# A second group of seven in the last feed-forward's up product, with both groups' weight sums made in DRAM by accumulating transfers

## The chip, the cores and the metric

The kernel runs on one core of a Trainium2 chip. The metric is the device time of one launch in microseconds (us), lower is better. Each kernel is run several times, and the median is given with the lowest and the highest.

## The reference

A two-layer encoder trunk on 256 rows of 1024 numbers, in float32. Each layer adds half a gated feed-forward, a token mixer (a causal depthwise convolution in the first layer, latent attention in the second), and another half feed-forward; an RMSNorm stands before each and at the end. There are four feed-forwards in all, and the last one is where the change lies.

```python
D_MODEL, SEQ, DEPTH, D_FF, FFN_RES_WEIGHT = 1024, 256, 2, 2816, 0.5

def rmsnorm(x, g):
    return x * lax.rsqrt(jnp.mean(x * x, axis=-1, keepdims=True) + RMS_EPS) * g

def swiglu_ffn(h, w1, w3, w2):
    return (jax.nn.silu(h @ w1) * (h @ w3)) @ w2

def reference(x, ...):
    h = x
    for i in range(DEPTH):
        h = h + FFN_RES_WEIGHT * swiglu_ffn(rmsnorm(h, ffn_norm1[i]), ffn1_w1[i], ffn1_w3[i], ffn1_w2[i])
        m = rmsnorm(h, mix_norm[i])
        h = h + (conv_module(m, ...) if i == 0 else mla(m, positions, ...))
        h = h + FFN_RES_WEIGHT * swiglu_ffn(rmsnorm(h, ffn_norm2[i]), ffn2_w1[i], ffn2_w3[i], ffn2_w2[i])
    return rmsnorm(h, final_norm)
```

## The kernel before, in words

**Numbers in two parts.** TensorE multiplies with operands of type fp32r, which hold fewer bits than float32. The kernel writes each float32 operand as a high part, the value cast to fp32r, and a low part, the rest. A product is three matmuls: rows high by weight low, high by high, low by high (`mm3`, lines 330 to 336; the three matmul lines are L332, L335 and L336).

**Weight blocks.** Weights come from DRAM in blocks of 128 x 2048 float32 (1 MB). A list, `blocks`, holds the order of use; `load` (L218) fetches the next block with a transfer of SyncE's queue (SP) into one of four `raw` buffers, ScalarE casts it to `hi` in two halves (L246) and VectorE subtracts to `lo` in two halves (L247). There are five pairs of `hi` and `lo`. `weights` hands out the next block and calls `load_ahead`, which has already written out the loads of the next three (four within a group of seven). Which instruction stands where in an engine's queue is decided when the kernel is built, by a scheduler with priorities; at run time each engine takes its queue in that order.

**A feed-forward.** `ffn_in` (L834) goes over the 2816 columns in six chunks `c`: five of 512 and one of 256. An ordinary chunk has four blocks, two for the first matrix (m=0) and two for the second (m=1), and each block serves both halves of the rows (tb=0 and 1): 2 x 2 x 8 products of `mm3`, 96 matmuls. Then come for each tb the SiLU on ScalarE (L948), the gate's product on VectorE (L950), and `turn`: a 32x32 transpose on VectorE (L470), four stores to DRAM (L474) and one read back (L479) by SP, and the high and low parts `Gh` and `Gl` (L845).

**A group of seven.** Four blocks (two by two) times two by two of rows is eight products of 12 matmuls. With Strassen's scheme (Winograd's form) it is seven, of sums of rows by sums of blocks: 84 matmuls. `SEVEN_UP` says which chunks are done so: chunk 3 of feed-forwards 1, 2 and 3 (0 is the first, 3 the last). The down product has a group of seven too (`SEVEN_DOWN`). The parts of it:

- `load_seven` (L189) fetches the four blocks (`fetched`, L182), makes four sums of them on VectorE in the raw buffers (`sub` in L204 to L210, recorded at its inner line L200), and splits each of the seven operands by L214 (ScalarE) and L200 (VectorE).
- `whole_rows` (L349) adds the rows' high and low parts, `sums_of_rows` (L344) makes four sums of them, and `forms_of` splits those (L361, L362). This runs two chunks before the group.
- `seven_products` (L366) runs the products in order and adds them up in four accumulators, with copies by ScalarE and two additions by VectorE (both recorded at the helper's line L258).

Instructions called through `urgent` get a high priority, and `behind` (L158) places a group's casts, subtractions and sums after the last six urgent ones of their engine. The gate's products of a chunk in `seven_up`, and of the chunk before it, are urgent. `fetched` and `load` place a load behind the last store that was placed so (`turns`).

**The ends of the stage before.** The MLA mixer's norms leave their last GpSimd operation at L1454; the norm of the last feed-forward has its last one at L519, `rh`, half the factor by which the down product's result is added. The final norm's operations (L724) come behind the down product.

## Time and profile before

| | |
|---|---|
| median of 3 runs | 900.82 us (898.79, 901.63, 900.82) |
| the profiled execution's own time | 902.66 us |
| its span in the trace | 900.9 us, mean granted clock 0.998 |
| TensorE busy | 890.0 us, 99% |
| VectorE busy | 743.2 us, 83% |
| ScalarE busy | 571.8 us, 63% |
| GpSimd busy | 104.9 us, 12% |
| transfers | 198.94 MB, mean 221 GB/s; SP's queue takes 61.2% of the 16 engines' span |

The table is from one profiled execution. The span runs from the first to the last recorded instruction; the execution's own time has the start and end around it. Busy shares are means over the whole span, while the change touches one stretch of it: the last feed-forward begins at about 730 us and its down product ends shortly before the final norm's operation at 888.15. Times in quoted rows are microseconds from the start of the span. A row of a timeline gives the start, the length, the engine, the line, the operation, output and inputs, the count (a row with x2 joins two instructions that follow each other), and in brackets the idle time before it with what ended it.

### The profile page before, as it was taken

What the parts mean: (1) busy time and instruction counts of PE and PEld (TensorE: products, weight loads), DVE (VectorE), ACT (ScalarE), POOL (GpSimd) and SP (SyncE); (2) the same over time, 40 slices, a digit from 0 to 9 for tenths busy, and PEclk for the clock granted to TensorE, in tenths of its full rate; (3) what the DMA queues carried; (4) which work ended last, traced back from release to release, by engine and by line L of the source; (5) the groups of instructions that cost most, each with busy time, mean ns of one, the idle gap of its engine ahead of it and who ended that gap; (6) DMA issues with size and microseconds to landing.
All of it is one profiled execution on the core that took longest, in us unless ns stands there. A gap on an engine that the chain in (4) does not pass through costs nothing.

```text
span 900.9 us, 12238 instructions
## 1 busy us (share of the span) xinstructions
PE 890.0 (99%) x4221; PEld 745.7 (83%) x4221; DVE 743.2 (83%) x1083; ACT 571.8 (63%) x993; POOL 104.9 (12%) x227
## 2 busy tenths in 40 slices
PE   9999999999999999999999999999999999999997
PEld 7888887898988888878888888788899888888886
DVE  6787779579998998899588989994768579999963
ACT  7966468388877645666375566564767576374752
POOL 1000000069962000000010000000400010000000
PEclk9999999999999999999999999999999999999999
DMA  9987629734315864939759369396545449377451
GB/s 333 363 313 282 212 69 335 295 125 171 105 57 207 291 241 154 368 98 356 283 167 331 136 206 354 98 384 219 198 165 178 150 141 352 99 287 293 169 200 47
DMA packets 71054, 198.94 MB, mean 221 GB/s; under 512 B 12368, under 2 KB 41936, under 8 KB 51664
## 3 DMA queue, kind: packets, MB, share of 16 engines
q1 hardware_dynamic: 70560, 197.47, 61.2%
q8 instruction: 33, 0.54, 0.2%
q10 hardware_dynamic: 432, 0.69, 0.2%
q14 instruction: 29, 0.24, 0.1%
HBM read 181.87 MB, written 16.25 MB: 220 GB/s over the span
## 4 chain that ended last, share of the span: by engine, by line
PE 82%; DVE 7%; DMA 6%; ACT 2%; issue 2%; SPq 0%; POOL 0%; DVEq 0%; ACTq 0%
PE u L336 13%; PE u L332 13%; PE u L335 13%; PE o L332 8%; PE o L336 8%; PE o L335 8%; PE u L993 3%; PE gate L993 3%; DVE lo L200 3%; DMA raw<-in_f1w 2%; PE u L403 2%; PE o L1229 2%; DMA raw<-in_f2w 2%; DVE raw L200 2%; DMA gd<-gt 1%
## 5 line engine op out<-in xcount | busy, mean ns | idle before, releaser
L247 DVE TENSOR_TENSOR lo<-raw,hi 128x1024 fp32r<-128x1024 f32 (+1 forms) x236 | 276.5, 1213 | 41.7 <-ACT hi L246 40.4
L246 ACT CAST hi<-raw 128x1024 fp32r<-128x1024 f32 (+1 forms) x238 | 236.5, 1044 | 89.1 <-DMA raw<-in_f2w 25.1
L332 PE MATMUL u<-lo,Xh 128*128 128x512 f32 x612 | 238.9, 390 | 0.3
L335 PE MATMUL u<-hi,Xh 128*128 128x512 f32 x612 | 238.4, 390 | 0.0
L336 PE MATMUL u<-hi,Xl 128*128 128x512 f32 x612 | 238.2, 390 | 0.0
L332 PEld LDWEIGHTS u<-lo,Xh 128*128 128x128 f32 x612 | 115.0, 188 | 25.3 <-DVE lo L200 1.6
L336 PEld LDWEIGHTS u<-hi,Xl 128*128 128x128 f32 x612 | 115.0, 188 | 24.5 <-DVE Xl L457 0.4
L335 PEld LDWEIGHTS u<-hi,Xh 128*128 128x128 f32 x612 | 115.0, 188 | 23.7
L214 ACT CAST hi<-raw 128x1024 fp32r<-128x1024 f32 x98 | 97.8, 1051 | 53.3 <-DVE raw L200 44.8
L200 DVE TENSOR_TENSOR lo<-raw,hi 128x1024 fp32r<-128x1024 f32 x98 | 116.0, 1217 | 6.4 <-ACT hi L214 6.3
L332 PE MATMUL o<-lo,Gh 128*128 128x512 f32 (+1 forms) x276 | 106.5, 388 | 0.4 <-DVE lo L200 0.4
L335 PE MATMUL o<-hi,Gh 128*128 128x512 f32 (+1 forms) x276 | 106.7, 387 | 0.0
L336 PE MATMUL o<-hi,Gl 128*128 128x512 f32 (+1 forms) x276 | 106.5, 386 | 0.0
L429 POOL TENSOR_TENSOR ms<-ss 128x1 f32<-128x1 f32 x16 | 8.1, 510 | 603.9 <-ACT junk L421 603.9
L200 DVE TENSOR_TENSOR raw<-raw,raw 128x2048 f32<-128x2048 f32 x28 | 63.8, 2280 | 3.9 <-DMA raw<-in_f2w 1.9
L332 PEld LDWEIGHTS o<-lo,Gh 128*128 128x128 f32 x276 | 51.9, 188 | 11.6 <-DVE lo L200 1.3
L336 PEld LDWEIGHTS o<-hi,Gl 128*128 128x128 f32 x276 | 51.9, 188 | 10.5
L335 PEld LDWEIGHTS o<-hi,Gh 128*128 128x128 f32 x276 | 51.9, 188 | 10.3
L1082 DVE SCALAR_TENSOR_TENSOR acc<-V,dw,acc 128x128 f32<-128x128 f32 (+1 forms) x174 | 53.9, 392 | 0.0
L1103 ACT ACTIVATE prod<-V,dw 128x128 f32<-128x128 f32 (+1 forms) x128 | 45.5, 415 | 1.8 <-POOL Y L1104 1.0
L845 ACT CAST Gh<-gb 128x512 fp32r<-128x512 f32 (+1 forms) x32 | 18.1, 567 | 39.2 <-DMA gb<-gd 39.2
L789 DVE SCALAR_TENSOR_TENSOR h<-o,rh,h 128x512 f32<-128x512 f32 (+1 forms) x18 | 12.9, 719 | 29.6 <-PE o L336 29.6
(265 smaller groups left out, 1274.6 us busy)
## 6 DMA issues: line engine op xcount, KB each, us to landing
raw<-in_f2w SPq DMA_DIRECT2D x66, 1024.0 KB, 6.3
raw<-in_f1w SPq DMA_DIRECT2D x62, 1024.0 KB, 6.6
raw<-in_cw SPq DMA_DIRECT2D x12, 1024.0 KB, 5.0
gd<-gt SPq DMA_DIRECT2D x160, 64.0 KB, 3.0
gb<-gd SPq DMA_DIRECT2D x24, 256.0 KB, 2.8
rows<-gd SPq DMA_DIRECT2D x16, 256.0 KB, 4.7
raw<-in_wo SPq DMA_DIRECT2D x4, 1024.0 KB, 4.8
hd<-rows SPq DMA_DIRECT2D x56, 64.0 KB, 2.2
```

What stands on the lines that cost most here:

```text
L200: ins = nc.vector.tensor_sub(out, left, right)
L214: casts[n, i] = nc.scalar.copy(hi[:, c], raw[:, c]), sub(lo[:, c], raw[:, c], hi[:, c].bitcast(F32))
L246: casts[len(loaded), i] = (nc.scalar.copy(hi[:, c], raw[:, c]), low.tensor_sub(lo[:, c], raw[:, c], hi[:, c].bitcast(F32)))
L247: low.tensor_sub(lo[:, c], raw[:, c], hi[:, c].bitcast(F32)))
L332: mm = nc.tensor.matmul(o, ah, bl, start=start, stop=False, skip_group_check=seeded)
L335: nc.tensor.matmul(o, ah, bh, start=False, stop=False, skip_group_check=seeded)
L336: return nc.tensor.matmul(o, al, bh, start=False, stop=stop, skip_group_check=seeded)
L403: mm = nc.tensor.matmul(o, al if kind == "x" else ah, bl if kind == "l" else bh, start=start and n == 0, stop=stop and n == len(kinds) - 1)
L845: gates.append((nc.scalar.copy(gh, bv), nc.vector.tensor_sub(low, bv, gh.bitcast(F32))))
L993: mm = nc.tensor.matmul(u[:, t], w[:, c], X.x[:, k, t], start=(k == 0), stop=(k == KT - 1))
L1082: dve_last.append(nc.vector.scalar_tensor_tensor(out if j == j1 - 1 else y, v, w, y, op0=ALU.mult, op1=ALU.add))
L1103: prods_last.append(nc.scalar.activation(p, v, AF.Copy, scale=w))
```

## The change

Chunk 2 of the last feed-forward becomes a group of seven like chunk 3. For both groups the four sums of weight blocks are no longer made by VectorE in the raw buffers. `seven_in_dram` makes four tiles in DRAM for each group, and `sums_in_dram` fills them with transfers of GpSimd's queue: a plain copy of one block, then a transfer that adds another block to it. The first call issues two copies and two additions for each group, behind the last norm operation of MLA (`last_pool[-1]`, L1454); the second call, in chunk 1, issues the same number behind the norm's last operation (`X.last_pool`, L519): a copy of a sum, and an addition to it. All sixteen are placed one behind the other in GpSimd's queue. The seven operands, four of them from these tiles, then are ordinary blocks of the list: each is loaded once by `load` and split by L246 and L247 (in the changed file L278 and L277). Since a transfer can only add, the signs of the sums change: `load_seven` adds where it subtracted, `sums_of_rows` swaps two operations, and `seven_products` subtracts in its two add-ups. That holds for every group in the kernel. The rows' sums now are made in chunk 1.

```diff
-SEVEN_UP = {1: (3,), 2: (3,), 3: (3,)}
+SEVEN_UP = {1: (3,), 2: (3,), 3: (2, 3)}
+IN_DRAM = {(3, 2), (3, 3)}
...
+    def seven_in_dram(four):
+        sums = [dram.tile([P, HB], F32, name=uid("sums")) for _ in range(4)]
+        in_dram.append((four, sums))
+        return [four[0], sums[0], sums[1], four[2], sums[2], four[3], sums[3]]
+
+    def sums_in_dram(then, after):
+        def queue(to, src, **kw):
+            nonlocal after
+            dma = nc.gpsimd.dma_start(to, src, **kw)
+            order(dma, after.ins)
+            after = dma
+
+        for four, sums in in_dram if not then else ():
+            queue(sums[0], four[1], max_dma_last_dim=4 * HB)
+            queue(sums[2], four[1], max_dma_last_dim=4 * HB)
+        for four, sums in in_dram if not then else ():
+            queue(sums[0], four[0], accum_op=ALU.add, max_dma_last_dim=4 * HB)
+            queue(sums[2], four[3], accum_op=ALU.add, max_dma_last_dim=4 * HB)
+        for n, of, added in ((1, 0, 3), (3, 1, 2)) if then else ():
+            for four, sums in in_dram:
+                queue(sums[n], sums[of], max_dma_last_dim=4 * HB)
+            for four, sums in in_dram:
+                queue(sums[n], four[added], accum_op=ALU.add, max_dma_last_dim=4 * HB)
...
-                    blocks += seven(four)
+                    blocks += (seven_in_dram if (n_ffn, cc_) in IN_DRAM else seven)(four)
...
         if j == 1:
-            sub(b[11], b[12], b[11])
-            sub(b[12], b[22], b[12])
+            sub(b[11], b[12], b[11], ALU.add)
+            sub(b[12], b[22], b[12], ALU.add)
         elif j == 2:
-            sub(b[11], b[22], b[11])
+            sub(b[11], b[22], b[11], ALU.add)
         elif j == 6:
-            sub(b[11], b[21], b[11])
+            sub(b[11], b[21], b[11], ALU.add)
...
-        sums = [(0, x22, x21, x22, ALU.add), (2, x21, x11, x21, ALU.subtract), (1, x11, x22, x11, ALU.subtract),
-                (3, x12, x12, x11, ALU.subtract)]
+        sums = [(0, x22, x21, x22, ALU.subtract), (2, x21, x11, x21, ALU.subtract), (1, x11, x22, x11, ALU.subtract),
+                (3, x12, x12, x11, ALU.add)]
...
-        add = urgent(nc.vector.tensor_add)(c12, c21, kept)
+        add = urgent(nc.vector.tensor_sub)(c12, kept, c21)
...
-        add = urgent(nc.vector.tensor_add)(c22, c21, kept)
+        add = urgent(nc.vector.tensor_sub)(c22, kept, c21)
...
-                nc.gpsimd.tensor_scalar(r, self.r[tb], 0.5, None, op0=ALU.mult)
+                self.last_pool = nc.gpsimd.tensor_scalar(r, self.r[tb], 0.5, None, op0=ALU.mult)
...
+            if c == 1 and later:
+                sums_in_dram(True, X.last_pool)
-            if seven_up and c == min(seven_up) - (1 if X.whole else 2):
+            if seven_up and c == max(1, min(seven_up) - (1 if X.whole else 2)):
                 forms = forms_of(sums_of_rows(*whole_rows(X.xh, X.xl)), Gh[:, 14:], Gl[:, 14:])
...
-            nc.gpsimd.tensor_tensor(rr, r2, R[tb], op=ALU.mult)
+            last_pool.append(nc.gpsimd.tensor_tensor(rr, r2, R[tb], op=ALU.mult))
...
+        sums_in_dram(False, last_pool[-1])
         part, = weights()
```

More of the change, by code (lines that the diff above doesn't have):

```diff
@@ L120, in seven @@
         return [("seven", j, four, group) for j in range(7)]
+    in_dram = []
+    def seven_in_dram(four):
[19 more added lines that the diff above has]
+                queue(sums[n], four[added], accum_op=ALU.add, max_dma_last_dim=4 * HB)
     blocks = []
@@ L198, in load_seven, with sub @@
             b[21] = fetched(four[2])
-        def sub(out, left, right):
-            ins = nc.vector.tensor_sub(out, left, right)
+        def sub(out, left, right, op=ALU.subtract):
+            ins = nc.vector.tensor_tensor(out, left, right, op=op)
             behind(ins)
@@ L831, in ffn, with ffn_in @@
         with tc.tile_pool(name=uid("ffn"), bufs=1) as act:
-            return ffn_in(act, X, make_next, beside, apart, SEVEN_UP.get(n, ()), n in SEVEN_DOWN)
-    def ffn_in(act, X, make_next, beside, apart, seven_up, seven_down):
+            return ffn_in(act, X, make_next, beside, apart, SEVEN_UP.get(n, ()), n in SEVEN_DOWN,
+                          (n, min(SEVEN_UP.get(n, (0,)))) in IN_DRAM)
+    def ffn_in(act, X, make_next, beside, apart, seven_up, seven_down, later):
         first_form = {}
@@ L1430, in mla_in @@
         last_low = [None]
+        last_pool = []
         def low(parts, w, tb, last):
```

## The prediction, made before the changed kernel had run

> **What bounds the kernel now.** I read the busy shares first, then the last feed-forward in stretches, then the chain of waits through its group of seven, then the queues of VectorE, ScalarE, GpSimd and the transfers.
>
> ```profile
> span 900.9 us, 12238 instructions
> PE 890.0 (99%) x4221; PEld 745.7 (83%) x4221; DVE 743.2 (83%) x1083; ACT 571.8 (63%) x993; POOL 104.9 (12%) x227
> ```
>
> TensorE is busy for 99% of the span, so a matmul less is worth its issue interval, if nothing else comes late. The stretches of the last feed-forward (columns: length, then busy time and count of TensorE, its weight loads, VectorE, ScalarE, GpSimd; clock; share of the transfer engines; GB/s):
>
> ```profile
> core 0: us, PE busy (x) PEld busy (x) DVE busy (x) ACT busy (x) POOL busy (x), PEclk, DMA share, GB/s
> 742.00:764.00 22.00, 22.00 (x98) 18.22 (x97) 20.25 (x24) 13.94 (x18) 0.00 (x0) 1.00 0.92 351
> 764.00:786.00 22.00, 22.00 (x99) 18.23 (x98) 21.80 (x24) 10.64 (x13) 0.00 (x0) 1.00 0.37 125
> 786.00:806.00 20.00, 19.90 (x88) 16.18 (x87) 18.11 (x20) 13.60 (x17) 0.00 (x0) 1.00 0.68 234
> 806.00:828.00 22.00, 22.00 (x99) 18.23 (x98) 21.96 (x21) 13.77 (x16) 0.00 (x0) 1.00 0.93 364
> 828.00:839.00 11.00, 11.00 (x51) 9.10 (x50) 10.07 (x12) 4.74 (x6) 0.00 (x0) 1.00 0.37 102
> 839.00:858.00 19.00, 19.00 (x85) 15.77 (x84) 19.00 (x22) 13.99 (x20) 0.00 (x0) 1.00 0.58 217
> ```
>
> 97 intervals in 22 us make 0.2268 us a matmul. VectorE is busy for 111.2 of these 116 us: it is as tight as TensorE here, and TensorE does not wait only because VectorE runs ahead. The chain of waits shows the one place where that lead ends, late in the seven of chunk 3 (start, us, what):
>
> ```profile
> 794.35 0.68 DVE Gl L845
> 795.03 0.96 DVE lo L200
> ...
> 796.08 2.29 DVE raw L200
> 798.37 1.14 DVE lo L200
> 799.50 0.60 DVE Gl L845
> 800.10 0.37 DVE u L258
> ...
> 800.62 1.23 DVE lo L200
> ...
> 801.89 0.50 PE u L332
> ```
>
> For 7.5 us the chain lies on VectorE; TensorE waits some 0.3 us for the low half of the seventh block. So the place that the change touches is bound by two engines at once, and the order in VectorE's queue decides.
>
> **The change, part by part.** I number the weight blocks of the last feed-forward as the changed kernel uses them: 0 to 7 are chunks 0 and 1, 8 to 14 the new seven of chunk 2, 15 to 21 that of chunk 3, 22 to 25 chunk 4, 26 and 27 chunk 5, 28 to 34 the seven of the down product.
>
> *TensorE.* Chunk 2 goes from 8 x 12 to 7 x 12 matmuls: 12 x 0.2268 = 2.7 us less.
>
> *The amount on VectorE and ScalarE.* These rows give intervals, from one start to the next:
>
> ```profile
> 735.59 2.28 DVE L349 TENSOR_TENSOR xs<-Xh,Xl 128x2048 f32<-128x2048 f32 x1
> ...
> 766.62 2.32 DVE L200 TENSOR_TENSOR lo<-raw,hi 128x1024 fp32r<-128x1024 f32 x2
> 768.97 4.62 DVE L200 TENSOR_TENSOR raw<-raw,raw 128x2048 f32<-128x2048 f32 x2
> 773.51 2.35 DVE L200 TENSOR_TENSOR lo<-raw,hi 128x1024 fp32r<-128x1024 f32 x2
> ...
> 776.98 2.29 DVE L200 TENSOR_TENSOR raw<-raw,raw 128x2048 f32<-128x2048 f32 x1
> ...
> 780.52 1.22 DVE L200 TENSOR_TENSOR lo<-raw,hi 128x1024 fp32r<-128x1024 f32 x1
> ...
> 782.25 1.22 DVE L200 TENSOR_TENSOR lo<-raw,hi 128x1024 fp32r<-128x1024 f32 x1
> ...
> 812.11 6.87 DVE L247 TENSOR_TENSOR lo<-raw,hi 128x1024 fp32r<-128x1024 f32 x6
> ...
> 821.28 2.29 DVE L200 TENSOR_TENSOR raw<-raw,raw 128x2048 f32<-128x2048 f32 x1
> 823.49 0.68 DVE L845 TENSOR_TENSOR Gl<-gb,Gh 128x512 fp32r<-128x512 f32 x1
> 824.10 0.68 DVE L950 TENSOR_TENSOR s<-s,u 128x512 f32<-128x512 f32 x1
> ```
>
> Half a block's low part takes (6.87 - 1.22) / 5 = 1.13 us, a sum of two blocks 2.2, a 128x512 operation 0.61. The changed signs turn additions into subtractions of the same shape and back; 735.59 is an addition and 821.28 a subtraction of the same length, so they cost nothing. VectorE loses four sums (-8.8) and gains three blocks (six halves, +6.8) and two additions of the second seven (+1.2): -0.8 us in all. ScalarE, idle a third of the time, gains three blocks and two copies.
>
> *The order on VectorE.* This is the step that decides. Before, VectorE writes the first three blocks of the seven (766.62, 773.51, 780.52 to 783.5) while chunk 2 is still running. In the changed kernel the instructions stand in VectorE's queue as follows (my list from the built program; a and b are the halves of a block's low part, T a gate's 32x32 transpose, mul a gate's product, sub an add-up of a seven):
>
> ```
> lo8 | mul(1,0) lo9a T lo9b mul(1,1) T lo10 lo11 sub(2) lo12 Gl sub(2) lo13 lo14a mul(2,0)
> lo14b T lo15 Gl mul(2,1) lo16a T lo16b Gl lo17a rows lo17b rows lo18a rows lo18b s1l sub(3)
> rows lo19 lo20 Gl sub(3) lo21 mul(3,0) Gl T lo22a
> ```
>
> mul(1,0) needs chunk 1's up half of the first rows, which TensorE finishes 12 matmuls before chunk 2. Everything behind it waits, so VectorE enters chunk 2 with one block and no more, where it entered chunk 3 with three. These rows fix the times:
>
> ```profile
> L335 PE MATMUL u<-hi,Xh 128*128 128x512 f32 x612 | 238.4, 390 | 0.0
> ...
> 732.92 5.78 ACT L246 CAST hi<-raw 128x1024 fp32r<-128x1024 f32 x6
> ...
> 788.28 0.57 ACT L258 COPY u<-u 128x512 f32<-128x512 f32 x1 [4.49 <-PE u L336]
> 788.76 2.00 ACT L214 CAST hi<-raw 128x1024 fp32r<-128x1024 f32 x2
> ```
>
> ScalarE sees chunk 3's first product at 788.28. A product takes 12 x 0.2268 = 2.72, and its last matmul ends 0.39 - 0.23 = 0.16 after the next may start; with 0.1 for the handing over, chunk 3 begins at 785.3, chunk 2 (96 matmuls earlier) at 763.5, and mul(1,0) may start at 763.5 - 2.7 + 0.2 = 761.0. From there to the first half of block 22 the queue holds 27 halves and 24 short operations: 27 x 1.13 + 24 x 0.61 = 45.1 us. It also waits inside. lo10: its cast stands behind ScalarE's copy of the first product (763.5 + 2.7 + 0.2, copy 0.5, half a cast 0.95 by (5.78 - 1.05) / 5, so 768.0, against 765.7 when VectorE is free): 2.3. lo11, behind the second product's copy: 0.5. The second sub(2), which needs the fifth product (lo12a at 774.8, so 777.8) while the sixth block's low part stands behind it: 1.3. mul(2,0), which needs the sixth product: 0.8. Together 4.9, so lo22a is written at 761.0 + 45.1 + 4.9 = 811.0. Before, chunk 4 began at 801.89 + 2.72 = 804.6. **+6.4 us** at chunk 4, with the 2.7 already in it.
>
> That a queue holds its order while later work is ready, the row 788.28 shows: ScalarE stood 4.49 us for the product though the cast behind it had its block summed since 773.5 and, with chunk 2 over, a free buffer from 785.3.
>
> *Chunks 4, 5 and the down product.* In chunk 4 a block serves 24 matmuls, 5.4 us against VectorE's 2.3, so nothing is lost; 144 matmuls bring the down product to 811.0 + 32.7 = 843.7. There VectorE now sums its blocks later, and ScalarE's copy of the first product stands behind three casts of the row sums (1.6), a SiLU (0.4), four half casts (3.8) and a gate's cast (0.5), the first of which waits for chunk 5's end at 843.9: copied at 850.8, against 849.2 when the third product could begin: **+1.7**. From 847.2 on VectorE's queue holds nine halves, a sum and 2.8 us of short work up to the seventh block (862.4), against 861.8: **+0.6**. Behind that the blocks serve 24 matmuls again.
>
> *Transfers.* GpSimd's queue:
>
> ```profile
> 651.39 0.19 POOL L1454 TENSOR_TENSOR rr<-r,R 128x1 f32<-128x1 f32 x1
> 721.73 0.20 POOL L429 TENSOR_TENSOR ms<-ss 128x1 f32<-128x1 f32 x1 [70.15 <-ACT junk L421]
> ...
> 727.06 0.22 POOL L519 TENSOR_SCALAR rh<-R 128x1 f32<-128x1 f32 x1
> 888.15 0.21 POOL L724 TENSOR_SCALAR fe<-fq 128x1 f32<-128x1 f32 x1 [160.86 <-ACT junk L718]
> ```
>
> The first eight transfers follow 651.6; the four accumulating ones wait for the copies, and behind them stand the norm's operations of 721.73, 70 us later. The second eight follow 727.3, with 160 us before the next operation. Both gaps are cover: if the first were used up, the norm's factor, and with it the SiLU of chunk 0, would come late one for one. On SP's queue the loads of the sums wait for GpSimd's transfers, and behind them stand the gates' stores and the weight loads that follow. The last link is the sum of all four for block 14: copy, add, copy, add after 727.3, wanted when VectorE reaches lo14a (780.7), less a half cast and a load, about 773. No row shows a transfer from DRAM to DRAM or an accumulating one; the nearest are loads of the same size (count, KB, us to landing; the second row is the quiet stretch 640 to 720):
>
> ```profile
> raw<-in_f2w SPq DMA_DIRECT2D x66, 1024.0 KB, 6.3
> ...
> raw<-in_f2w SPq DMA_DIRECT2D x7, 1024.0 KB, 4.8
> ```
>
> Four links of one quiet load each end at 746; pairs that share the engines, and twice that for an addition, which reads its target too, make 2 x 12.6 + 2 x 25.2 = 75.6 and end at 803, 30 us late. I take 0, by the nearer row (4 x 6.3 ends at 752), and keep 0 to +30. The six more weight loads cost nothing while they land within 8 us, since VectorE's queue is later than they are.
>
> The Trainium skill (SBUF — State Buffer, section "SBUF: two separate sides") says that GpSimd writes the descriptors of its own transfers and is locked out while VectorE runs an instruction that takes the second port. It speaks against the change; but it names copies, and the stretch here holds two-input operations, and no run here shows GpSimd's transfers yet. If each of the second eight waited for one sum of 2.28 us, 18 us would go, which alone still leaves 752 + 18 = 770.
>
> **Sum.** 902.66 (the profiled execution's own time) + 6.4 + 1.7 + 0.6 = 911.4. The median of the runs is 1.84 lower, so I forecast 909.6.
>
> **The rivals.** *The sums come late* (the change does not make them ahead of time): SP's queue stops at block 14's load and TensorE with it, one for one from 773 on. For it: the window 742 to 764 has its transfer engines at 0.92 already, and the eight transfers come on top. Against: 46 us for four links. At 10 us late the time is 919.6; at the bound 939.6. The Trainium skill (DMA: Bandwidth & Descriptors, section "Issuing engines are not separate DMA queues") says that transfers of all issuers run on the same 16 engines and interleave, which is this rival's premise.
>
> *Faster: VectorE keeps its lead.* If VectorE wrote the low parts of blocks 9 to 12 before 761.0, TensorE would stay the bound and the whole 2.7 us would be saved: 898.1. For it: in amount VectorE has 0.8 us less to do. Against: mul(1,0) stands ahead of lo9 in a queue that keeps its order. Each half written before 761.0 gives back 1.13 us, so the sign turns at eight halves; around that point lies *no change*, 898 to 903.5.
>
> **How the numbers follow.** VectorE's order as worked out, with the sums in time: 0.64. Late sums 0.18, no change 0.10, faster 0.08. 0.3% is 2.7 us, about what a measurement of this kernel can tell from no change: faster 0.08, same 0.10, slower 0.82. The range leaves out the faster case (0.08), the lower part of no change (0.04) and sums more than 16 us late (0.08, of a lateness spread evenly from 0 to 30): 901 to 926.
>
> **What would show it.** Right: 12 matmul rows fewer than the 4,221 of the page; VectorE idle for about 4 us before 761; in chunk 2's stretch, TensorE waiting about 2 us for the low part of the sixth block; TensorE waiting on low halves through chunk 3, for about 9 us in all from 763 to 811; chunk 4 about 6.4 us later than before. Wrong: TensorE without gaps until chunk 4 (then the faster rival holds), one long wait on the load of block 14's sum, or GpSimd's first eight transfers running past 721 (then the late sums).

## The result, and the profile after

The changed kernel takes 923.72 us (median; 920.99 to 924.21) against 901.23 us (898.79 to 902.00) for the kernel before on the same chip: a ratio of 1.0241, 95% interval 1.0221 to 1.0261, so 22.5 us slower. I had forecast 909.6 (8.7 slower), with 901 to 926 as the range and 0.82 on slower. The direction and the range held, the size did not.

The profiled execution of the changed kernel took 920.99 us, the fastest of its four and 18.3 more than that of before; the accounts below are of these two. From its page, the span, the busy shares, the queue of GpSimd's transfers (count of packets, MB, share of the 16 engines' span) and two rows of the transfers (count, KB, median us to landing):

```profile
span 918.9 us, 12270 instructions
PE 893.7 (97%) x4209; PEld 742.3 (81%) x4209; DVE 742.8 (81%) x1087; ACT 578.6 (63%) x1001; POOL 115.5 (13%) x243
q0 software_dynamic: 2304, 16.78, 6.8%
sums<-in_f2w POOLq DMA_DIRECT2D x12, 1024.0 KB, 14.9
raw<-sums SPq DMA_DIRECT2D x8, 1024.0 KB, 8.6
```

The twelve matmuls are gone (4,221 to 4,209), and VectorE has no less to do (743.2 to 742.8). The stretches of the last feed-forward, same columns as in the prediction, with a short one ahead:

```profile
736.00:739.00 3.00, 2.92 (x7) 2.34 (x8) 2.90 (x5) 3.00 (x7) 0.67 (x1) 0.50 1.02 220
742.00:764.00 22.00, 22.00 (x99) 18.23 (x98) 14.29 (x18) 9.01 (x13) 2.73 (x4) 1.00 1.01 332
764.00:786.00 22.00, 17.50 (x75) 13.56 (x74) 14.62 (x16) 11.56 (x15) 0.00 (x0) 1.00 1.03 343
786.00:806.00 20.00, 16.70 (x65) 11.27 (x64) 18.39 (x21) 14.31 (x18) 0.00 (x0) 1.00 0.98 368
806.00:828.00 22.00, 19.57 (x82) 14.89 (x82) 22.00 (x25) 15.45 (x18) 0.00 (x0) 1.00 0.98 350
```

Two things differ from before. TensorE has gaps from 764 to 828. And the transfer engines, 0.92, 0.37, 0.68 and 0.93 busy in these four stretches before, are full in all of them, while VectorE in 764 to 786 is busy for 14.6 us of 22 instead of 21.8: it now waits too. The chain of waits of the changed kernel says for what (start, us, what):

```profile
732.95 10.54 DMA gd<-gt
...
743.95 12.31 DMA raw<-in_f2w
...
756.34 1.06 ACT hi L277
...
757.42 2.37 DVE lo L278 x2
...
759.81 16.08 DMA raw<-sums
...
775.91 1.05 ACT hi L277
...
776.98 1.24 DVE lo L278
...
778.26 0.50 PE u L363
```

From 733 to 776 the chain is a gate's store, a load of a block and a load of a sum, 39 us of 43 on transfers. None of the three waits for a sum that isn't ready: the load at 743.95 goes once the gate's stores are in, and the one at 759.81 once VectorE has given its raw buffer back (SP waits behind 759.79, the end of `lo`). They are only slow: a block landed after 6.3 us in the median before, and the six loads that go out between 743 and 766 now take 12 to 22. GpSimd's queue (timeline) shows what is running beside them:

```profile
650.56 2.33 POOL L136 DMA_DIRECT2D sums<-in_f2w  x4
...
679.31 0.82 POOL L136 DMA_DIRECT2D sums<-in_f2w  x1 [10.68 <-issue]
720.80 0.19 POOL L460 TENSOR_TENSOR ms<-ss 128x1 f32<-128x1 f32 x1 [40.67 <-ACT junk L452]
...
726.41 1.18 POOL L136 DMA_DIRECT2D sums<-sums  x2
732.69 0.89 POOL L136 DMA_DIRECT2D sums<-in_f2w  x1 [5.09 <-DMA sums<-sums]
...
745.23 0.54 POOL L136 DMA_DIRECT2D sums<-sums  x1 [8.56 <-DMA sums<-in_f2w]
750.49 0.53 POOL L136 DMA_DIRECT2D sums<-sums  x1 [4.71 <-DMA sums<-in_f2w]
755.15 0.83 POOL L136 DMA_DIRECT2D sums<-in_f2w  x1 [4.13 <-DMA sums<-sums]
760.04 0.83 POOL L136 DMA_DIRECT2D sums<-in_f2w  x1 [4.07 <-DMA sums<-sums]
```

The first eight are done long before the norm (the last one lands at 699.4), whose first operation comes at 720.80 (721.73 before), so that cover held. The second eight run from 726.4 to about 773, the whole approach to the new seven.

**Where the 18 us lie.** I take the start of chunk 0 and of chunk 4 from the first matmul of each. Chunk 0 starts at 719.6 before (not at about 730, as I had put the feed-forward's beginning) and 718.7 after (-0.9). From there to chunk 4 is 85.1 us before and 101.5 after (+16.4). From chunk 4 to the end of the span is 96.1 before and 98.7 after (+2.6). Of the +16.4, 5.0 lie ahead of chunk 2 and 11.4 between chunk 2 and chunk 4 (41.2 to 52.6).

### The profile page after: what moved, and what is told of

Its sections match the earlier page's. It is cut to its first block, busy times and chain, and to the rows that moved or that the text cites. A ratio compares the mean times of both kernels' runs of the same rounds, so it can differ in the third digit from the quotient of the medians.

```text
span 918.9 us, 12270 instructions
## 1 busy us (share of the span) xinstructions
PE 893.7 (97%) x4209; PEld 742.3 (81%) x4209; DVE 742.8 (81%) x1087; ACT 578.6 (63%) x1001; POOL 115.5 (13%) x243
## 3 DMA queue, kind: packets, MB, share of 16 engines
HBM read 204.94 MB, written 33.03 MB: 259 GB/s over the span
## 4 chain that ended last, share of the span: by engine, by line
PE 70%; DVE 12%; DMA 11%; issue 4%; ACT 2%; SPq 1%; DVEq 0%; ACTq 0%
PE u L363 10%; PE u L367 10%; PE u L366 10%; PE o L363 7%; PE o L366 7%; PE o L367 7%; DVE lo L231 4%; DMA raw<-in_f2w 4%; PE u L1027 3%; PE gate L1027 3%; DMA gd<-gt 3%; PE o L1263 2%; PE u L434 2%; DVE lo L278 2%; DMA raw<-sums 2%
## 5 line engine op out<-in xcount | busy, mean ns | idle before, releaser
L278 DVE TENSOR_TENSOR lo<-raw,hi 128x1024 fp32r<-128x1024 f32 (+1 forms) x256 | 300.0, 1210 | 58.5 <-ACT hi L277 56.5
L277 ACT CAST hi<-raw 128x1024 fp32r<-128x1024 f32 x258 | 256.3, 1044 | 110.7 <-DMA raw<-in_f2w 36.7
L363 PE MATMUL u<-lo,Xh 128*128 128x512 f32 x592 | 232.2, 392 | 5.3 <-ACT Xh L621 3.2
L366 PE MATMUL u<-hi,Xh 128*128 128x512 f32 x592 | 230.9, 390 | 0.0
L367 PE MATMUL u<-hi,Xl 128*128 128x512 f32 x592 | 230.8, 390 | 0.0
L363 PEld LDWEIGHTS u<-lo,Xh 128*128 128x128 f32 x592 | 111.5, 188 | 32.3 <-DVE lo L278 4.4
L367 PEld LDWEIGHTS u<-hi,Xl 128*128 128x128 f32 x592 | 111.4, 188 | 24.2 <-DVE Xl L488 0.5
L245 ACT CAST hi<-raw 128x1024 fp32r<-128x1024 f32 x84 | 83.7, 1049 | 41.2 <-DVE raw L231 35.6
L231 DVE TENSOR_TENSOR lo<-raw,hi 128x1024 fp32r<-128x1024 f32 x84 | 99.3, 1214 | 4.8 <-ACT hi L245 4.6
L231 DVE TENSOR_TENSOR raw<-raw,raw 128x2048 f32<-128x2048 f32 x24 | 54.7, 2278 | 0.6 <-DMA raw<-in_f1w 0.4
L982 ACT ACTIVATE s<-u,R 128x512 f32<-128x512 f32 (+1 forms) x48 | 30.8, 647 | 12.3 <-PE u L367 7.3
```

The source lines that it names most:

```text
L231: ins = nc.vector.tensor_tensor(out, left, right, op=op)
L245: casts[n, i] = nc.scalar.copy(hi[:, c], raw[:, c]), sub(lo[:, c], raw[:, c], hi[:, c].bitcast(F32))
L277: casts[len(loaded), i] = (nc.scalar.copy(hi[:, c], raw[:, c]), low.tensor_sub(lo[:, c], raw[:, c], hi[:, c].bitcast(F32)))
L278: low.tensor_sub(lo[:, c], raw[:, c], hi[:, c].bitcast(F32)))
L363: mm = nc.tensor.matmul(o, ah, bl, start=start, stop=False, skip_group_check=seeded)
L366: nc.tensor.matmul(o, ah, bh, start=False, stop=False, skip_group_check=seeded)
```

## The experiments

Each was timed on one chip with the kernel before, whose median there was 901.9 to 902.5. Two theories stood after the result: *order* (what I had forecast, VectorE's queue) with *late sums* as its rival, and *contention* (the second eight transfers delay every other transfer). The first four runs take parts away.

**e1: no transfers, plain blocks in place of the sums.**

```diff
-        return [four[0], sums[0], sums[1], four[2], sums[2], four[3], sums[3]]
+        return [four[0], four[1], four[3], four[2], four[1], four[3], four[0]]
...
-                sums_in_dram(True, X.last_pool)
...
-        sums_in_dram(False, last_pool[-1])
```

> All sixteen of GpSimd's transfers are left out; where a sum was loaded, one of the plain weight blocks of the same size is loaded, so TensorE, VectorE, ScalarE and SP's queue have the work of the changed kernel (the values of chunks 2 and 3 are wrong). Contention theory (the second eight transfers, from 726 to 773 us, take the transfer engines from the norm's rows, the gates' stores and the weight loads): the 13.6 us that the changed kernel lost beyond the forecast go, 905 to 912 us. Queue theory (the whole 22 us are the order on VectorE): 918 to 924 us. The scheduler plans anew without the transfers, so some instructions of the stretch stand in another order on VectorE and ScalarE; where the plan itself held the loss, the time falls below 905.

907.29, ratio 1.0062 (1.0041 to 1.0082). Without the transfers three quarters of the loss are gone. But the scheduler, with the transfers gone, gave VectorE another order (the waits of TensorE are one of 2.7 us on a low part and one of 2.3 on an add-up, where the changed kernel has seven on low parts), so neither the part that is gone nor the part that is left can be put down to one cause. e7 mends that.

**e2: the first eight alone**, the second call dropped.

```diff
-        sums = [dram.tile([P, HB], F32, name=uid("sums")) for _ in range(4)]
+        sums = [dram.tile([P, HB], F32, name=uid("sums")) if n % 2 == 0 else four[3 - n] for n in range(4)]
...
-                sums_in_dram(True, X.last_pool)
```

> The first eight transfers (650 to 700 us) stay, the second eight are left out, and plain blocks are loaded in place of the two sums that they make (values of chunks 2 and 3 wrong). Contention in the last feed-forward alone: as the run without any transfers, within 1.5 us. If the first eight cost something too, in the mixer's end: 2 us or more above it.

906.49, ratio 1.0058 (1.0037 to 1.0078), the same as e1 within the intervals. The two runs have different orders on VectorE, so this alone does not clear the first eight; but in all traces except e7's and e8's chunk 0 starts between 717.7 and 719.9 us, with the first eight or without them (e7, with them, has 716.2). So up to there they cost nothing that can be seen; what the second eight cost, e5 and e7 show.

**e3: one seven only** (chunk 3, its sums in DRAM).

```diff
-SEVEN_UP = {1: (3,), 2: (3,), 3: (2, 3)}
-IN_DRAM = {(3, 2), (3, 3)}
+SEVEN_UP = {1: (3,), 2: (3,), 3: (3,)}
+IN_DRAM = {(3, 3)}
```

> Only chunk 3 is a group of seven, as before the change, with its four sums made in DRAM: eight transfers in all, four of them from 726 us on, and VectorE has four sums (8.8 us) less to do than before. Contention theory: the norm's rows still come late (the two first copies start with them), 903 to 908 us, slower than before. Queue theory: VectorE has more room than before, 898 to 901.5 us.

905.66, ratio 1.0044 (1.0027 to 1.0060). With half as many transfers the norm costs TensorE 0.3 us; its longest wait, 2.9, is on a gate's product in the down product, a place where the scheduler's plan differs. That wait belongs to neither theory, so the run does not tell them apart. It says that the same number of matmuls as before, with sums from DRAM and the scheduler's new order, is 0.4% slower than sums on VectorE.

**e4: both sevens, all sums on VectorE**, so no transfers.

```diff
-IN_DRAM = {(3, 2), (3, 3)}
+IN_DRAM = set()
```

> Two groups of seven, and VectorE makes all eight sums, as it makes those of the other feed-forwards; no transfers of GpSimd. VectorE has 8 x 2.2 = 17.6 us more than in the run without any transfers, in a stretch where it has no room: 10 to 17 us above that run (some 918 to 926 us) if VectorE's queue bounds the stretch; within 3 us of it if it does not.

914.98, ratio 1.0149 (1.0126 to 1.0173), 7.7 us above e1: between the two expectations. TensorE waits 11.9 us on low parts, 8.0 of it at one place. Its order on VectorE is another one again, so the 7.7 us are not the price of the sums alone; VectorE is busy for 759.7 us against 742.0 in e1, and that load the change does take from it.

**e5: all sixteen transfers run, and nothing reads them.** The two calls stay, and from chunk 0 on TensorE, VectorE, ScalarE and SP have the order of the changed kernel, instruction for instruction.

```diff
-        return [four[0], sums[0], sums[1], four[2], sums[2], four[3], sums[3]]
+        return [four[0], four[1], four[3], four[2], four[1], four[3], four[0]]
```

> All sixteen transfers run where the changed kernel has them, but nothing reads their sums: plain blocks of the same size are loaded in their place (values of chunks 2 and 3 wrong). The order on every engine and queue is that of the changed kernel. Contention theory: as the changed kernel, 921 to 925 us. Theory of late sums (loads wait until the sums are made): the time falls to that of the run without transfers, 905 to 910 us.

923.42, ratio 1.0235 (1.0211 to 1.0259), the time of the changed kernel. Nothing waits for a sum here, so the late sums are refuted. The transfers cost what they cost by running.

**e6: the second eight's four additions become plain copies**, with the order of the changed kernel.

```diff
-                queue(sums[n], four[added], accum_op=ALU.add, max_dma_last_dim=4 * HB)
+                queue(sums[n], four[added], max_dma_last_dim=4 * HB)
```

> The four adding transfers of the second eight are plain copies of the same block instead (two sums of each group hold a plain block: values wrong); orders as in the changed kernel. If an adding transfer takes more of the transfer engines than a copy (the trace has 12 to 14 us against 6 to 9.5), the loss shrinks by a third to a half: 912 to 918 us. If only the count of transfers matters: 921 to 925 us.

918.17, ratio 1.0171 (1.0146 to 1.0196), 5.3 us less than e5 on the same chip, a quarter of the loss where a third to a half was expected. An addition costs more than a copy, and eight copies still cost 6.0 us over e7, which has the same order and next to no traffic.

**e7: the changed kernel's order without the load.** The second eight move 64 of 2048 columns, nothing reads them, and the instructions of TensorE, VectorE, ScalarE and SP are chained in the order of the changed kernel.

```diff
-        return [four[0], sums[0], sums[1], four[2], sums[2], four[3], sums[3]]
+        return [four[0], four[1], four[3], four[2], four[1], four[3], four[0]]
...
-            dma = nc.gpsimd.dma_start(to, src, **kw)
+            part = slice(None) if not then else slice(64)
+            dma = nc.gpsimd.dma_start(to[:, part], src[:, part], **kw)
...
+    for numbers in PLAN:    # the instructions of one engine, in the changed kernel's order
+        names = [f"I-{n}" for n in numbers.split()]
+        for a, b in zip(names, names[1:]):
+            tc.add_manual_dep(traced[b], a, ...)
```

> The second eight transfers move 64 of the 2048 columns and nothing reads any sum (values of chunks 2 and 3 wrong), but the order on TensorE, VectorE, ScalarE and SP's queue in the last feed-forward is held to that of the changed kernel by explicit dependencies. This is the case that the forecast worked out, without its transfers: 908 to 912 us by the forecast's walk through VectorE's queue. If the plan is innocent: as the run planned anew, 905 to 908 us. If the plan alone holds the loss: 918 us or more.

912.15, ratio 1.0104 (1.0087 to 1.0121). This splits the loss in two: 9.7 us are the order, with the saved matmuls already in it, and the 11.3 us up to e5, which has the same order, are the transfers' traffic. (By the intervals of the ratios a difference of two runs is good to some 3 us.) What the traffic does is seen in two answers of the transfers' view for 742 to 766 (count, KB, median us to landing). The changed kernel:

```profile
raw<-in_f2w SPq DMA_DIRECT2D x3, 1024.0 KB, 17.3
raw<-sums SPq DMA_DIRECT2D x3, 1024.0 KB, 16.1
...
gd<-gt SPq DMA_DIRECT2D x4, 64.0 KB, 19.0
```

e7:

```profile
raw<-in_f2w SPq DMA_DIRECT2D x4, 1024.0 KB, 5.2
gd<-gt SPq DMA_DIRECT2D x12, 64.0 KB, 2.4
```

Loads take three times as long, and a gate's store of 64 KB, 2.4 us in e7, takes 19.

**e8: the transfers earlier.** The whole kernel, with the first eight spread over the gates of chunks 1 and 3 in feed-forwards 1 and 2, and the second eight in the mixer.

```diff
+            if not then:
+                first_half.append((to, src, kw))
+                return
...
-                sums_in_dram(True, X.last_pool)
...
+                if n_ffns[0] in (2, 3) and c in (1, 3) and first_half:
+                    to, src, kw = first_half.pop(0)
+                    tick = small.tile([P, 1], F32, tag="tick", name=uid("tick"))
+                    after = nc.gpsimd.tensor_tensor(tick, s[:, :1], s[:, :1], op=ALU.mult)
+                    order(nc.gpsimd.dma_start(to, src, **kw), after.ins)
...
-        sums_in_dram(False, last_pool[-1])
+        sums_in_dram(True, last_pool[-1])
```

> A whole kernel: the sums as in the change, but earlier. The first eight transfers are spread over the gates of chunks 1 and 3 of the second and third feed-forward, one behind each gate, and the second eight stand where the first eight stood, in the mixer. Contention theory: as the run without any transfers, 905 to 909 us, if the spread ones cost nothing where they are now; up to 914 us if those stretches have no room either.

924.98, ratio 1.0239 (1.0219 to 1.0260): nothing won, against the expectation of the contention theory. But the time is lost at other places: chunk 0 of the last feed-forward starts at 737.7 us, 19.0 later than in the changed kernel. From there to chunk 4 e8 needs 87.0 us where the changed kernel needs 101.5, and TensorE has three gaps of over 0.25 us in the rest of the span (2.25, 0.33 and 0.52), so with the transfers over before it begins, its loads come in time. In 500 to 600, the third feed-forward, TensorE's waits are

```profile
PE o L368 <- DVE lo L236: 4.7, 1, 4.7
PE u L368 <- DVE s L294: 2.3, 1, 2.3
PE o L368 <- DVE s L988: 1.0, 1, 1.0
```

where the changed kernel has TensorE busy for 99.7 us of that 100 (e8: 91.9, at a granted clock of 0.95). The longest of them falls where the transfer engines are at 0.35:

```profile
586.00:592.00 6.00, 1.34 (x7) 0.82 (x5) 6.00 (x10) 4.61 (x6) 0.00 (x0) 0.86 0.35 102
592.00:596.00 4.00, 4.00 (x10) 3.13 (x11) 4.00 (x5) 4.00 (x6) 0.00 (x0) 0.50 0.25 66
```

VectorE is busy for all 6 us there. With the eight small products that start the transfers (four of them in this stretch) the scheduler made another plan, and VectorE's queue has another order than in the changed kernel; that this order is the cause is argued from the busy VectorE and the free transfer engines, and not shown. So the run does not say what the change costs with its transfers early and its plan kept; that stays open.

**e9: e5, with the second eight held until VectorE has written the norm's last low rows**, the order chained as in e7.

```diff
+    tc.add_manual_dep(traced["I-6919"], "I-6814", ...)    # the first held transfer, the last of the rows
```

> As the run whose sums nothing reads (all sixteen transfers at full size, plain blocks loaded, values of chunks 2 and 3 wrong), but the second eight wait until VectorE has written the low rows of the norm; the order on TensorE, VectorE, ScalarE and SP's queue is held to that of the changed kernel. If the wait for the norm's rows adds to the rest: 5 us less than the run with the transfers at once, 917 to 919.5 us. If the later waits take it back, since VectorE only used the stall to get ahead: 921 to 925 us.

925.00, ratio 1.0254 (1.0217 to 1.0290). TensorE's stall in chunk 0 is gone, and three others of 3.2, 2.0 and 3.0 us stand in chunk 2 instead. Held back by 7 us (the first goes out at 733.9, in e5 at 727.0), the traffic costs the same.

**e10: the sums on GpSimd itself**, in the raw buffers, in halves, for both groups.

```diff
-IN_DRAM = {(3, 2), (3, 3)}
+IN_DRAM = set()
...
+            if op == ALU.add and b["pool"]:
+                for i in range(PIECES):
+                    c = slice(i * HB // PIECES, (i + 1) * HB // PIECES)
+                    nc.gpsimd.tensor_tensor(out[:, c], left[:, c], right[:, c], op=op)
+                return
```

> A whole kernel: both groups of seven in the last feed-forward, no transfers of sums, and GpSimd makes all eight sums in SBUF, each in two halves. The nearest row of GpSimd's additions, 0.74 us for 128x256 in the convolution, makes 5.9 us a sum. Contention theory with VectorE's order: no transfers, so 904 to 909 us like the run planned anew without any, if GpSimd keeps up; 910 to 918 us if its 23.6 us a group bound the group's 19.0 us on TensorE.

933.11, ratio 1.0346 (1.0309 to 1.0383), the slowest of all and beyond both expectations. Groups of VectorE and GpSimd in 740 to 840 (count, then busy us and mean ns of one):

```profile
L234 POOL TENSOR_TENSOR raw<-raw,raw 128x1024 f32<-128x1024 f32 x16 | 45.0, 2825 | 55.0 <-DVE lo L236 55.0
...
L236 DVE TENSOR_TENSOR lo<-raw,hi 128x1024 fp32r<-128x1024 f32 x28 | 46.3, 1696 | 6.0 <-ACT hi L250 6.0
```

A half of a low part takes 1696 ns in the mean; the changed kernel's take 1213 in the same view. The timeline of VectorE shows which of its operations slow down:

```profile
795.61 2.86 DVE L398 TENSOR_TENSOR s1l<-rows,s1h 128x512 fp32r<-128x512 f32 x1
...
798.39 0.68 DVE L294 TENSOR_TENSOR s<-s,u 128x512 f32<-128x512 f32 x1
```

Two operations of the same size: the one with both inputs in SBUF takes 2.86 us instead of 0.68, the gate's product, one of whose inputs is in PSUM, does not. The Trainium skill (SBUF — State Buffer, section "SBUF: two separate sides") says that VectorE, with two inputs in SBUF, and a GpSimd operation that reads SBUF take a shared pair of ports by turns, each for a whole instruction. The two rows agree: GpSimd's additions run from 791.8 to 803.4, beside both. How much of the 31 us this makes, and how much GpSimd's own pace, the run does not say.

**e11: half in DRAM, half on GpSimd.** The first eight stay in the mixer; the other two sums of each group are made by GpSimd in SBUF (the last of them adds another pair of blocks than the change's, so its value differs).

```diff
-                sums_in_dram(True, X.last_pool)
...
+        if "sums" in b:
+            for to, added in {2: ((1, 2),), 6: ((4, 3),)}.get(j, ()):
+                for i in range(PIECES):
+                    c = slice(i * HB // PIECES, (i + 1) * HB // PIECES)
+                    nc.gpsimd.tensor_tensor(b[to][:, c], b[to][:, c], b[added][:, c], op=ALU.add)
```

> A whole kernel: the first eight transfers stay in the mixer, where leaving out the second eight showed them to cost nothing, and the other two sums of each group, which the second eight made, are made by GpSimd in SBUF (2 x 5.9 us a group by the convolution's row). 903 to 909 us, as the run with the first eight alone; below 899 us, and so faster than before, only if VectorE's order no longer makes TensorE wait.

917.67, ratio 1.0173 (1.0132 to 1.0215), where 903 to 909 was expected: less than the change loses, and still far behind the kernel before; TensorE waits 12.9 us on low parts.

**e12: a better order, without the load.** e7 with VectorE's queue rewritten: the low parts of blocks 9 and 10 ahead of chunk 1's gate product, those of 12 and 13 ahead of the two add-ups, 14 and 16 ahead of chunk 2's gate products, and the row sums behind block 25; ScalarE's casts follow. (VectorE's line of the list, numbers of instructions; 7012 to 7022 are the halves of blocks 9 and 10, 7075 to 7090 chunk 1's gate.)

```diff
-    "... 6956 7075 7012 7077 7014 7088 7090 7020 7022 7108 7110 7166 7129 7131 ..."
+    "... 6956 7012 7014 7020 7022 7075 7077 7088 7090 7108 7110 7129 7131 7166 ..."
```

> As the run that keeps the changed kernel's plan without its transfers (values of chunks 2 and 3 wrong), with the plan edited by hand: on VectorE the low parts of blocks 9 and 10 stand ahead of chunk 1's first gate product, that of block 12 ahead of the first add-up, that of block 13 ahead of the second, the second half of block 14 ahead of chunk 2's first gate product and block 16 ahead of its second; the sums of the gates' rows are moved behind block 25; ScalarE's casts follow (blocks 10 and 11 ahead of the copy of the first product, 12 ahead of the second). The forecast said that each half written before chunk 1's gate product gives back 1.13 us and that the place of the low parts behind gate products and add-ups makes the 6.4 us at chunk 4. If so, TensorE's 8.2 us of waits up to chunk 4 shrink by 5 to 8 us: 903.5 to 907 us against 912.15. If the amount of work on VectorE, and not its order, makes the waits: 910 us or more.

905.27, ratio 1.0036 (1.0023 to 1.0048), 6 us less than e7 by the ratios. From chunk 2 to chunk 4 it takes 42.7 us where e7 takes 47.8. So the lead that VectorE doesn't have is indeed what e7 pays for there: the position in the queue, and not the amount of work, which is equal.

**e13: the change with e12's order**, sums read (the edit is shown against e12).

```diff
-        return [four[0], four[1], four[3], four[2], four[1], four[3], four[0]]
+        return [four[0], sums[0], sums[1], four[2], sums[2], four[3], sums[3]]
...
-            part = slice(None) if not then else slice(64)
-            dma = nc.gpsimd.dma_start(to[:, part], src[:, part], **kw)
+            dma = nc.gpsimd.dma_start(to, src, **kw)
```

> A whole kernel: the change as it is, sums read and all sixteen transfers at full size, with the hand-edited plan of the run before (VectorE ahead by the low parts of blocks 9 and 10 at chunk 1's gate product). If contention adds to the order's cost: 905.3 plus the 11.5 us between the changed kernel and the run that keeps its plan, 915 to 919 us. If VectorE's lead hides the late loads: 905 to 909 us. If the loads of the sums, which the edited plan wants sooner, come late one for one: 920 us or more.

924.06, ratio 1.0238 (1.0214 to 1.0263): nothing left of the 6 us. The chain of waits says why:

```profile
728.11 8.82 DMA rows<-hd
...
743.24 11.92 DMA raw<-in_f2w
...
758.71 16.71 DMA raw<-sums
...
775.50 1.05 ACT hi L285
...
778.94 0.61 DVE s L297
```

Block 10's load lands at 775.4, as in the changed kernel (775.9). A better queue cannot get past a block that isn't there; the gate's product now stands behind that block's low part, and TensorE waits one product earlier, 7.8 us at once.

## Why the prediction was right in its direction and wrong in its size

**Right: the amount of work.** 12 matmuls less, and VectorE's total unchanged (-0.4 us on the page).

**Right: the order on VectorE, term by term.** In e7, where the order is that of the changed kernel and the traffic is gone, VectorE's timeline shows each wait that I had put into the sum:

```profile
757.61 0.69 DVE L298 TENSOR_TENSOR s<-s,u 128x512 f32<-128x512 f32 x1 [4.14 <-PE u L376]
...
764.67 2.36 DVE L287 TENSOR_TENSOR lo<-raw,hi 128x1024 fp32r<-128x1024 f32 x2 [2.17 <-ACT hi L286]
767.33 2.36 DVE L287 TENSOR_TENSOR lo<-raw,hi 128x1024 fp32r<-128x1024 f32 x2 [0.30 <-ACT hi L286]
...
774.52 0.70 DVE L298 TENSOR_TENSOR u<-p,u 128x512 f32<-128x512 f32 x1 [1.36 <-PE u L376]
...
779.45 0.69 DVE L298 TENSOR_TENSOR s<-s,u 128x512 f32<-128x512 f32 x1 [0.84 <-PE u L376]
```

Forecast: idle about 4 ahead of mul(1,0), then 2.3, 0.5, 1.3 and 0.8. Measured: 4.14, 2.17, 0.30, 1.36 and 0.84. From chunk 0 to chunk 4 e7 needs 91.75 us (716.2 to 807.95) against 85.15 before: +6.6 where I had +6.4. From chunk 4 to the end it needs 98.7 against 96.1: +2.6 where I had 1.7 + 0.6. The median of e7 is 9.7 us above that of before, against 8.7; its profiled execution, 908.78 us, is the fastest of its four by 3.3, and starts chunk 0 3.4 us earlier than that of before. The last two of these terms stand in the changed kernel as well (+2.6), and so do the later waits in chunk 3: TensorE's waits of 720 to 880 there are

```profile
PE u L363 <- DVE lo L278: 9.7, 7, 2.9
PE u L363 <- ACT Xh L621: 3.2, 1, 3.2
```

The 9.7 us on low parts look like the 9 us forecast, but they are not the same waits: 2.9 and 1.6 of them belong to the loads of blocks 10 and 9. In e7 the same view has 5.5 us, and 9.7 only with all the smaller pauses (47.8 us from chunk 2 to chunk 4, less 168 intervals of 0.2268). That the view's total in the changed kernel meets the forecast is chance.

**Right: the first eight, and the norm's operations on GpSimd.** The row at 720.80 shows that the cover held, and e2 that they cost nothing up to chunk 0.

**Wrong: the step "Transfers", where I took 0.** I had worked out when the sum for block 14 would be ready, and took 752. Its addition went out at 755.15 and landed 11.9 us later, at 767.0 (the last one, for block 21, at about 773), and its load went out only at 782.4 (SP's timeline):

```profile
782.40 0.37 SPq L269 DMA_DIRECT2D raw<-sums  x1
```

So the links were slower than I took them, between my two ends, and the sum was still 15 us early: to the question that I asked, 0 was the right answer. But it was the wrong question. I asked when the *sums* would be ready, and not what their making does to the other transfers, though I had quoted 0.92 for the transfer engines in that very stretch. The sentence that six more loads "cost nothing while they land within 8 us" named the condition, and it failed: the loads of 743 to 766 landed after 12 to 22. Where the sum has 0, the price is 11.3 us (e5 less e7), of which additions instead of copies are 5.3 (e5 less e6). It has two places in the changed kernel. The first is the norm: the second half of the rows is read back from DRAM behind the first copies, and ScalarE waits for it (timeline, the same instruction before and after):

```profile
731.74 1.28 ACT L590 ACTIVATE Xh<-rows,G 128x128 fp32r<-128x128 f32 x4 [2.60 <-DMA rows<-hd]
```

```profile
735.63 1.28 ACT L621 ACTIVATE Xh<-rows,G 128x128 fp32r<-128x128 f32 x4 [7.62 <-DMA rows<-hd]
```

TensorE stands 3.4 us for it, and then runs some of chunk 0 at half clock (the window 736 to 739), 5 us in all. The second is the load of blocks 9 and 10, 4.8 us between chunk 2 and chunk 4 beyond e7 (52.6 against 47.85). Together 9.8 of the 12.2 between the two profiled executions; the rest, 2.5, is a lead that e7's has when chunk 0 starts (716.2 against 718.7), which no experiment places. Nor does one tell whether the transfer engines themselves set the pace or the DRAM behind them.

**The rivals.** *Late sums* had the right premise, that the eight transfers come on top of engines already at 0.92, and the wrong victim: SP's queue does not stop at block 14's load; everything that uses the engines gets slower from 727 on. e5 refutes the mechanism. The Trainium skill (DMA: Bandwidth & Descriptors, section "Issuing engines are not separate DMA queues"), which I had named beside this rival, says that transfers of all issuers share 16 engines; the loads' median of 5.2 us in e7 and 16 to 17 in the changed kernel agree, and had I taken the rule for the loads, and not for the sums alone, the term would not have been 0. *VectorE keeps its lead* is refuted: it enters chunk 2 with one block, as listed. Of what I had cited from the Trainium skill (SBUF — State Buffer, section "SBUF: two separate sides") against the change, GpSimd locked out of writing descriptors, the trace shows no sign: the issues took 0.5 to 0.9 us each, and those of the second eight that waited went out 0.4 us after the landing they waited for. The order term and the traffic term are not two independent costs, as e12 and e13 show: with the traffic, the order of e12 is worth nothing.

**The bound on the range** that held (926) came from late sums of up to 16 us, a mechanism that did not occur. That it held is luck.

None of the thirteen variants beat the kernel before. The best, e12, leaves the making of the sums out and is still 0.36% slower.

## What to carry to other kernels

Work moved into transfers is not free where the transfer engines are near full: price it as traffic, with every load and store that runs beside it, the small ones on the critical chain first, and ask what they take before asking whether the moved work is ready in time. Where two engines are tight, what counted here is which instruction stands ahead of which in an in-order queue; a list of that queue with durations from the profile gave each wait to within 0.2 us. And a scheduler makes another plan as soon as a part is taken away, so to separate two causes, keep the plan fixed and take away the load only.

## What the runs showed of the hardware that I had not expected

- Among the second eight, an accumulating transfer of 1 MB from DRAM to DRAM took 12 to 14 us beside loads and stores, a plain copy 6 to 9.5. With up to four of the first eight under way at once it took longer: 7 to 20 us a copy, 20 to 24 an addition. Once only additions were left of these, from 672.3 on, the transfer engines are counted as full at a lower rate than with copies among them (changed kernel, stretches of the mixer, last two columns share and GB/s):

```profile
660.00:670.00 10.00, 10.00 (x70) 9.22 (x70) 5.25 (x8) 5.00 (x13) 1.66 (x2) 1.00 0.98 380
670.00:680.00 10.00, 10.00 (x72) 9.43 (x71) 6.32 (x20) 9.64 (x22) 0.69 (x1) 1.00 1.05 273
```

The pages' counts of DRAM traffic (read 181.87 MB before and 204.94 after, written 16.25 and 33.03) grow by the sixteen transfers and the six more loads once each, so whatever an addition reads of its target is not in them.

- A stall of TensorE can cost half as much again afterwards (stalls here are from one matmul's start to the next, less the 0.23 us of an interval, which is some 0.2 us more than the waits' view lists): behind the 3.4 us at 736 the granted clock is 0.50 for some 3 us (1.6 us lost). After 3.1 us at 778 it stays at 1.00, and in e1 after 2.5 us at 796 too, but after 2.8 us at 805 it is 0.55. A stall of 2.1 us ahead of the sixth block of chunk 2 is common to the changed kernel, e5, e6 and e7: the clock stays at 1.00 behind it in three of them, and is 0.70 and 0.73 in the two stretches of 3 us behind it in e6 (787 to 793). The Trainium skill (TensorE: Matmul & The Clock Gate, section "Part 1: The HAM clock gate (the "warmup" mystery)") says that the clock is halved after about one idle window of 3.4 us, and that the window runs freely. That these stalls don't sort by length agrees with a window that runs freely; that stalls of 2.8 and 2.1 us were enough goes against the figure, and here the measurement decides.
- GpSimd's additions in SBUF took more from VectorE than they did for it. In e10 they kept GpSimd busy for 45.0 us (sixteen halves), and VectorE's busy time on the page is 768.5 us: 26.5 more than in e1, which has as many VectorE instructions (1087) and makes no sums, and 8.8 more than in e4, where VectorE makes the eight sums itself.
